# Matmul, causal mask and softmax: longer runs over four batches, and the mask read as 2.5 KB runs behind the weight

## The chip, the cores and the metric

The kernel runs on one core of a Trainium2 chip. The metric is the device time of one execution in microseconds (us); lower is better. Ten executions of the kernel before took 90.90 to 91.21 us, median 90.98. A profile of one execution (90.9 us) gives the instructions of each engine and the work of the core's 16 DMA engines.

Names: TensorE (PE) multiplies, and its weight loads are listed apart (PEld); VectorE is DVE, ScalarE is ACT, GpSimd is POOL, SyncE is SP. In this kernel every DMA is issued by SP, so all of them stand in one queue.

## The reference

```python
batch, m, k, n = 16, 512, 512, 512
x = randn(16, 512, 512); weight = randn(512, 512); scale = 0.125
mask = (np.triu(np.ones((m, n))) == 0)      # 1 strictly below the diagonal

y = scale * np.matmul(x, weight)
y = np.where(mask == 1, y, -1e9)
y_exp = np.exp(y - np.max(y, axis=-1, keepdims=True))
out = y_exp / np.sum(y_exp, axis=-1, keepdims=True)
```

All tensors are float32 in memory. x and the output are 16 MB each, the weight is 1 MB, and so is the whole mask. Row r of a batch has r columns that count. The first row of each batch has none, so its softmax is 1/512 everywhere. For rows 0 to 255 the right half of the columns is masked out entirely.

## The kernel before, in words

**Units.** The work is cut into 16 units. A unit holds half of the rows (h = 0: rows 0 to 255, h = 1: rows 256 to 511) of two neighbouring batches. Each of its 128 partitions holds four neighbouring rows of one batch, a run of 8 KB in memory. So a unit's x tile is 1 MB, its output tile too. Units alternate between h = 0 and h = 1.

**Steps of a unit.** `load` (L78) reads the x tile. `cast` (L83) turns it to bf16 on DVE. `transpose` (L88) makes 16 transposes of 128x128 on PE into two PSUM tiles. `evict` (L101) copies one of them to SBUF on DVE and the other on ACT. `multiply` (L108) does, for each of four row slots, four matmuls with the bf16 weight and a fifth one that adds a band of the mask (an identity times `band`, L127); then ACT takes the exponential and the row's sum. For h = 0 only the left 256 columns are computed; the right half of those output tiles was zeroed once at the start. `normalise` (L148) divides on DVE, and POOL writes 1/512 to the first rows. `store` (L158) writes the output tile.

**The band.** The mask matters only in the four 128x128 squares on its diagonal. At the start these are read into `diag_f32`, one mask row of each square to a partition, as 512 pieces of 512 bytes. DVE turns ones and zeros into 0 and -512 (`diag_bf`, L194). Four matmuls with `spread` (L208) bring the rows to the partitions and slots where the units have them, and DVE and ACT copy them into `band` (L215), 256 columns wide.

**Order.** `seq` keeps the program's order on each engine. SP issues x of unit 0, the mask squares, the weight, then x of units 1 to 7. PE runs 12 matmuls on zeros first. Unit 0 is cast, transposed and evicted, the band is made, the weight is cast. Then the loop over u follows: transpose(u+1), cast(u+2), evict(u+1), multiply(u), normalise(u-1), store(u-1), and the load of unit u+7 into the x buffer that has come free. There are eight x buffers and eight output buffers of 8 KB a partition, three buffers each for the bf16 x and its transpose, and four PSUM banks for each of the two uses.

Of the kernel before, what the change touches and what calls it, by code (L numbers as in the profile page):

```python
# [8 lines left out]
FP32 = mybir.dt.float32  # L9
BF16 = mybir.dt.bfloat16  # L10
AF = mybir.ActivationFunctionType
ALU = mybir.AluOpType

MASK_NEG = -512.0
P = 128
X_BUFS = 8
OUT_BUFS = 8
WARM = 12


@with_exitstack
def kernel(
    ctx: ExitStack,
    tc: tile.TileContext,
    x: bass.AP,
    weight: bass.AP,
    scale: float,
    mask: bass.AP,
    out: bass.AP,
):  # L30

    nc = tc.nc

    B, M, K = x.shape
    K2, N = weight.shape
    assert K == K2 and N == 512 and K == 512 and M == 512 and B % 2 == 0
    KT = K // P
    T = 4
    HP = P // 2
    HB = 2 * P
    U = B  # L50

    const = ctx.enter_context(tc.tile_pool(name="const", bufs=1))
    x_pool = ctx.enter_context(tc.tile_pool(name="xf", bufs=X_BUFS))
    xb_pool = ctx.enter_context(tc.tile_pool(name="xb", bufs=3))
    xt_pool = ctx.enter_context(tc.tile_pool(name="xt", bufs=3))
    sum_pool = ctx.enter_context(tc.tile_pool(name="sums", bufs=4))
    psum_t = ctx.enter_context(tc.tile_pool(name="psum_t", bufs=4, space=bass.MemoryType.PSUM))
    psum_y = ctx.enter_context(tc.tile_pool(name="psum_y", bufs=4, space=bass.MemoryType.PSUM))

    x_r = x.rearrange("(c e) (h p t) k -> c h p e (t k)", e=2, h=2, t=T)  # L60
    out_r = out.rearrange("(c e) (h p t) n -> c h p e (t n)", e=2, h=2, t=T)

    diag_r = bass.AP(tensor=mask.tensor, offset=mask.offset, ap=[[N, P], [P * N + P, KT], [1, P]])

    ident_bf = const.tile([P, P], BF16, name="ident_bf")
    w_f32 = const.tile([P, KT, N], FP32, name="w_f32")
    w_bf = const.tile([P, KT, N], BF16, name="w_bf")
    diag_f32 = const.tile([P, KT, P], FP32, name="diag_f32")
    diag_bf = const.tile([P, KT, P], BF16, name="diag_bf")
    spread = const.tile([P, T, P], BF16, name="spread")  # L70
    zeros = const.tile([P, N], BF16, name="zeros")
    band = const.tile([P, 2, T, HB], BF16, name="band")
    ots = [const.tile([P, T, N], FP32, name=f"ot{i}") for i in range(OUT_BUFS)]

    st_x, st_xb, st_pt, st_xt, st_sum = {}, {}, {}, {}, {}
    seq = tc.keep_in_program_order

    def load(u):  # L78
        xf = x_pool.tile([P, T, K], FP32, name="xf")
        seq(nc.sync.dma_start(xf.rearrange("p t k -> p (t k)"), x_r[u // 2, u % 2]))  # L80
        st_x[u] = xf

    def cast(u):  # L83
        xb = xb_pool.tile([P, T, K], BF16, name="xb")
        seq(nc.vector.tensor_copy(xb, st_x.pop(u)))  # L85
        st_xb[u] = xb

    def transpose(u):  # L88
        xb = st_xb.pop(u)
        st_pt[u] = [psum_t.tile([P, 2, T, P], BF16, name="pt") for _ in range(2)]  # L90
        for kt in range(KT):
            for t in range(T):
                seq(
                    nc.tensor.transpose(  # L94
                        st_pt[u][kt // 2][:, kt % 2, t],
                        xb[:, t].rearrange("p (k kt) -> p kt k", kt=KT)[:, kt],
                        ident_bf,
                    )
                )

    def evict(u):  # L101
        xt = xt_pool.tile([P, KT, T, P], BF16, name="xt")
        pt = st_pt.pop(u)
        seq(nc.vector.tensor_copy(xt[:, 0:2], pt[0]))  # L104
        seq(nc.scalar.copy(xt[:, 2:4], pt[1]))  # L105
        st_xt[u] = xt

    def multiply(u):  # L108
        h = u % 2
        NC = (h + 1) * HB  # L110
        xt = st_xt.pop(u)
        ot = ots[u % OUT_BUFS]
        rsum = sum_pool.tile([P, T], FP32, name="rsum")
        for t in range(T):
            py = psum_y.tile([P, N], FP32, name="py")
            for kt in range(KT):
                seq(
                    nc.tensor.matmul(  # L118
                        py[:, :NC],
                        lhsT=xt[:, kt, t],  # L120
                        rhs=w_bf[:, kt, :NC],
                        start=(kt == 0),
                        stop=(kt == KT - 1),
                    )
                )
            seq(
                nc.tensor.matmul(  # L127
                    py[:, h * HB : NC],
                    lhsT=ident_bf,
                    rhs=band[:, h, t],  # L130
                    start=False,
                    stop=True,
                    skip_group_check=True,
                )
            )
            seq(
                nc.scalar.activation(  # L137
                    out=ot[:, t, :NC],
                    in_=py[:, :NC],
                    func=AF.Exp,  # L140
                    bias=0.0,
                    scale=float(scale),
                    accum_out=rsum[:, t : t + 1],
                )
            )
        st_sum[u] = rsum

    def normalise(u):  # L148
        ot = ots[u % OUT_BUFS]
        NC = (u % 2 + 1) * HB  # L150
        rinv = sum_pool.tile([P, T], FP32, name="rinv")
        seq(nc.vector.reciprocal(rinv, st_sum.pop(u)))  # L152
        for t in range(T):
            seq(nc.vector.tensor_scalar_mul(ot[:, t, :NC], ot[:, t, :NC], rinv[:, t : t + 1]))  # L154
        if u % 2 == 0:
            seq(nc.gpsimd.memset(ot[0:2, 0, :HB], 1.0 / N))  # L156

    def store(u):  # L158
        ot = ots[u % OUT_BUFS]
        seq(nc.sync.dma_start(out_r[u // 2, u % 2], ot.rearrange("p t n -> p (t n)")))  # L160


    load(0)
    seq(nc.sync.dma_start(diag_f32, diag_r))  # L164
    seq(nc.sync.dma_start(w_f32, weight.rearrange("(p kt) n -> p kt n", kt=KT)))  # L165
    for u in range(1, X_BUFS):
        load(u)


    nc.vector.memset(zeros, 0.0)  # L170
    idle = psum_y.tile([P, N], FP32, name="py")
    for _ in range(WARM):
        seq(nc.tensor.matmul(idle, lhsT=zeros[:, :P], rhs=zeros, start=True, stop=True))  # L173

    make_identity(nc, ident_bf)
    nc.gpsimd.memset(band[:HP, :, :, P:], MASK_NEG)
    nc.gpsimd.memset(band[HP:, :, :, :P], 0.0)
    for i in range(0, OUT_BUFS, 2):
        nc.vector.memset(ots[i][:, :, HB:], 0.0)  # L179
        nc.gpsimd.memset(ots[i][0:2, 0, HB:], 1.0 / N)  # L180


    for g in range(2):
        for e in range(2):
            seq(
                nc.scalar.copy(  # L186
                    spread.rearrange("k t (g p e) -> k t g p e", g=2, e=2)[:, :, g, :, e],
                    ident_bf.rearrange("k (p t) -> k t p", t=T),
                )
            )  # L190

    cast(0)
    seq(
        nc.vector.tensor_scalar(  # L194
            out=diag_bf,
            in0=diag_f32,
            scalar1=-MASK_NEG,
            scalar2=MASK_NEG,
            op0=ALU.mult,
            op1=ALU.add,  # L200
        )
    )
    transpose(0)
    evict(0)
    for t in range(T):
        pm = psum_y.tile([P, N], FP32, name="py")
        seq(
            nc.tensor.matmul(  # L208
                pm, lhsT=spread[:, t], rhs=diag_bf.rearrange("k b c -> k (b c)"), start=True, stop=True
            )  # L210
        )
        for g, copy in enumerate((nc.vector.tensor_copy, nc.scalar.copy)):
            half = slice(g * HP, (g + 1) * HP)
            src = pm.rearrange("p (h g c) -> p h g c", h=2, g=2)
            seq(copy(band[half, :, t, g * P : (g + 1) * P], src[half, :, g]))  # L215
    seq(nc.vector.tensor_copy(w_bf[:, 0:2], w_f32[:, 0:2]))
    seq(nc.scalar.copy(w_bf[:, 2:4], w_f32[:, 2:4]))
    cast(1)

    for u in range(U + 1):  # L220
        if u + 1 < U:
            transpose(u + 1)
        if u + 2 < U:
            cast(u + 2)
        if u + 1 < U:
            evict(u + 1)
        if u < U:
            multiply(u)
        if u >= 1:
            normalise(u - 1)  # L230
            store(u - 1)
            if u - 1 + X_BUFS < U:
                load(u - 1 + X_BUFS)


# [33 lines left out]
```

The softmax here doesn't subtract the row's maximum and nothing guards it: scores larger than these inputs give would overflow.

## Time and profile before

| What | Value |
|---|---|
| Median of 10 executions | 90.98 us (90.90 to 91.21) |
| The profiled execution | 90.9 us |
| Its span, first to last instruction | 89.1 us |
| Busy: PE, DVE, ACT, POOL | 70.9, 60.4, 55.2, 7.3 us |
| Mean granted TensorE clock | 0.932 |
| DMA: bytes, mean rate over the span | 34.95 MB, 392 GB/s |
| x tiles: 16 loads of 1 MB, median from issue to landing | 14.2 us |
| Output: 16 stores of 1 MB, median from issue to landing | 11.0 us |
| Weight, 1 MB; mask squares, 256 KB: issue to landing | 8.5 us; 6.6 us |

The span leaves out what lies around the first and last instruction, 1.8 us in the profiled execution. In the page's slices a digit is a busy share in tenths. "DMA" is the mean busy share of the 16 DMA engines and "GB/s" what they moved in that slice. An issue-to-landing time includes the time in the queue behind other transfers.

### The profile page before, as it was taken

Reading aid. Unit: us, or ns where it says so; the run is one execution under the profiler, and the core shown is the slowest. Engines: PE = TensorE matmul, PEld = TensorE weight load, DVE = VectorE, ACT = ScalarE, POOL = GpSimd, SP = SyncE. Lnnn points to the kernel's source line nnn. Section 1 sums busy time; section 2 is a strip of 40 time slices with the busy share of each in tenths; the row PEclk is TensorE's granted clock in tenths of the full one; section 3 lists DMA queues with packets and bytes.
Section 4 is the critical chain, followed back from the end, with each engine's and each line's share of the span. In section 5 each row is a group of like instructions: output and inputs, shape, how many; then the busy total and the mean of one; then the engine's idle time right before and its main releaser. Section 6 shows DMA issues by size and latency. Waiting matters only on the chain.

```text
span 89.1 us, 1610 instructions
## 1 busy us (share of the span) xinstructions
PE 70.9 (80%) x584; PEld 49.1 (55%) x592; DVE 60.4 (68%) x123; ACT 55.2 (62%) x154; POOL 7.3 (8%) x20
## 2 busy tenths in 40 slices
PE   4966205999999999999999999999999999930000
PEld 1315005776598479659857964984796497400000
DVE  5875914758579949986994998698593976535000
ACT  5402930658687869687786977778787778650000
POOL 7620000002000200010020002002000100200000
PEclk9999975579999999999999999999999999999855
DMA  0969999999999999999999999999999999999960
GB/s 15 313 211 377 430 438 416 419 434 427 419 412 419 434 427 423 430 404 430 419 430 427 427 412 434 427 423 430 427 423 419 434 416 434 416 434 427 430 294 29
DMA packets 5286, 34.95 MB, mean 392 GB/s; under 512 B 544, under 2 KB 1056, under 8 KB 1056
## 3 DMA queue, kind: packets, MB, share of 16 engines
q1 hardware_dynamic: 5280, 34.87, 94.1%
q8 instruction: 4, 0.07, 0.3%
q14 instruction: 2, 0.02, 0.0%
HBM read 18.09 MB, written 16.78 MB: 391 GB/s over the span
## 4 chain that ended last, share of the span: by engine, by line
PE 72%; DMA 12%; DVE 3%; SPq 2%; issue 1%; ACT 1%; DVEq 0%; ACTq 0%
PE py L118 48%; PE pt L94 16%; DMA xf<-in_x_dram 12%; PE py L127 8%; DVE ot L154 1%; DVE xb L85 1%; SPq L80 1%; ACT ot L137 1%; SPq L164 1%; SPq L165 1%; DVEq L264 0%; DVE rinv L152 0%; ACTq L264 0%
## 5 line engine op out<-in xcount | busy, mean ns | idle before, releaser
L118 PE MATMUL py<-w_bf,xt 128*128 128x256 bf16 (+1 forms) x248 | 50.4, 331 | 0.4
L137 ACT ACTIVATE ot<-py 128x256 f32<-128x256 f32 (+1 forms) x64 | 31.2, 494 | 8.4 <-PE py L127 8.1
L118 PEld LDWEIGHTS <-xt 128*128 128x128 bf16 x256 | 25.0, 100 | 12.6
L105 ACT COPY xt<-pt 128x1024 bf16<-128x1024 bf16 x16 | 16.2, 1012 | 14.8 <-PE pt L94 10.2
L85 DVE CAST xb<-xf 128x2048 bf16<-128x2048 f32 x16 | 19.5, 1220 | 7.0 <-DMA xf<-in_x_dram 7.0
L154 DVE TENSOR_SCALAR ot<-ot,rinv 128x256 f32<-128x256 f32 (+1 forms) x64 | 23.5, 431 | 0.8
L94 PE MATMUL pt<-ident_bf,xb 128*128 128x128 bf16 x256 | 17.8, 225 | 6.0 <-DVE xb L85 6.0
L94 PEld LDWEIGHTS <-xb 128*128 128x128 bf16 x256 | 16.6, 115 | 7.8 <-DVE xb L85 6.9
L127 PE MATMUL py<-band,ident_bf 128*128 128x256 bf16 x64 | 17.7, 277 | 0.0
L104 DVE COPY xt<-pt 128x1024 bf16<-128x1024 bf16 x16 | 11.0, 687 | 7.4 <-PE pt L94 7.4
L137 ACT ACTIVATION_READ_ACCUMULATOR ot<-py 128x1 f32 x64 | 12.8, 200 | 0.0
L156 POOL MEMSET ot<- 2x256 f32 x8 | 3.6, 448 | 67.1 <-DVE ot L154 67.1
L127 PEld LDWEIGHTS <-ident_bf 128*128 128x128 bf16 x64 | 6.4, 100 | 4.3
L173 PE MATMUL py<-zeros 128*128 128x512 bf16 x12 | 4.8, 583 | 1.2 <-DVE zeros L170 1.2
L152 DVE RECIPROCAL rinv<-rsum 128x4 f32<-128x4 f32 x16 | 2.7, 169 | 3.2 <-ACT ot L137 3.2
L179 DVE MEMSET ot<- 128x1024 f32 x4 | 3.6, 912 | 0.6 <-issue 0.6
L173 PEld LDWEIGHTS <-zeros 128*128 128x128 bf16 x12 | 1.6, 140 | 3.9 <-issue 2.7
L186 ACT ACT_TABLE_LOAD x1 | 1.3, 1283 | 0.7 <-PEq L250 0.7
L215 ACT CAST band<-py 64x256 bf16<-64x256 f32 x4 | 1.4, 367 | 0.1
L215 DVE CAST band<-py 64x256 bf16<-64x256 f32 x4 | 1.4, 404 | 0.0
L180 POOL MEMSET ot<- 2x256 f32 x4 | 1.2, 302 | 1.5 <-DVE ot L179 1.4
L208 PE MATMUL py<-diag_bf,spread 128*128 128x512 bf16 x4 | 1.0, 377 | 0.3 <-DVE diag_bf L194 0.3
(14 smaller groups left out, 6.6 us busy)
## 6 DMA issues: line engine op xcount, KB each, us to landing
xf<-in_x_dram SPq DMA_DIRECT2D x16, 1024.0 KB, 14.2
out_dram<-ot SPq DMA_DIRECT2D x16, 1024.0 KB, 11.0
w_f<-in_weight_dram SPq DMA_DIRECT2D x1, 1024.0 KB, 8.5
diag_f<-in_mask_dram SPq DMA_DIRECT2D x1, 256.0 KB, 6.6
```

Of the source, the lines that this page charges most:

```text
L85: seq(nc.vector.tensor_copy(xb, st_x.pop(u)))
L94: nc.tensor.transpose(st_pt[u][kt // 2][:, kt % 2, t], xb[:, t].rearrange("p (k kt) -> p kt k", kt=KT)[:, kt], ident_bf,)
L104: seq(nc.vector.tensor_copy(xt[:, 0:2], pt[0]))
L105: seq(nc.scalar.copy(xt[:, 2:4], pt[1]))
L118: nc.tensor.matmul(py[:, :NC], lhsT=xt[:, kt, t], rhs=w_bf[:, kt, :NC], start=(kt == 0), stop=(kt == KT - 1),)
L127: nc.tensor.matmul(py[:, h * HB : NC], lhsT=ident_bf, rhs=band[:, h, t], start=False, stop=True, skip_group_check=True,)
L137: nc.scalar.activation(out=ot[:, t, :NC], in_=py[:, :NC], func=AF.Exp, bias=0.0, scale=float(scale), accum_out=rsum[:, t : t + 1],)
L154: seq(nc.vector.tensor_scalar_mul(ot[:, t, :NC], ot[:, t, :NC], rinv[:, t : t + 1]))
L156: seq(nc.gpsimd.memset(ot[0:2, 0, :HB], 1.0 / N))
L173: seq(nc.tensor.matmul(idle, lhsT=zeros[:, :P], rhs=zeros, start=True, stop=True))
L179: nc.vector.memset(ots[i][:, :, HB:], 0.0)
L215: seq(copy(band[half, :, t, g * P : (g + 1) * P], src[half, :, g]))
```

## The change

- A tile now holds eight neighbouring rows to a partition, a run of 16 KB, over four neighbouring batches: 2 MB for one h. A unit of compute is still 1 MB: four of the eight row slots of a tile. So two units with h = 0 are followed by two with h = 1. All x tiles but the first are loaded as one transfer of 2 MB; the first in two halves. All output tiles but the first and last are stored as one transfer, after the second unit; those two in halves. There are five x buffers and four output buffers, each of 16 KB a partition; the bf16 x and its transpose have two buffers instead of three.
- The queue at the start: first half of x tile 0, weight, second half of x tile 0, mask, then x tiles 1 to 4. The mask had been second.
- The mask is read in four transfers, one for each square. Each reads 64 runs of 2.5 KB: the 128 columns of one mask row, then on through memory to the 128 columns of the next row. Sixteen partitions get four runs each. The data lie for that time in the last output buffer. In all 640 KB are read instead of 256 KB, and into 64 partitions instead of 128.
- The band has two DVE conversions of 64 partitions (even and odd rows), four matmuls with a smaller `spread`, and eight copies of 64 partitions by 512 elements. It is made after units 0 and 1 were transposed and evicted, and after 14 and 8 more matmuls on zeros.

```diff
-X_BUFS = 8
-OUT_BUFS = 8
+X_BUFS = 5
+OUT_BUFS = 4
...
+    E = 4
+    S = 8
     T = 4
...
-    xb_pool = ctx.enter_context(tc.tile_pool(name="xb", bufs=3))
-    xt_pool = ctx.enter_context(tc.tile_pool(name="xt", bufs=3))
+    xb_pool = ctx.enter_context(tc.tile_pool(name="xb", bufs=2))
+    xt_pool = ctx.enter_context(tc.tile_pool(name="xt", bufs=2))
...
-    x_r = x.rearrange("(c e) (h p t) k -> c h p e (t k)", e=2, h=2, t=T)
-    out_r = out.rearrange("(c e) (h p t) n -> c h p e (t n)", e=2, h=2, t=T)
-    diag_r = bass.AP(tensor=mask.tensor, offset=mask.offset, ap=[[N, P], [P * N + P, KT], [1, P]])
+    x_r = x.rearrange("(c e) (h p t) k -> c h p e (t k)", e=E, h=2, t=S)
+    out_r = out.rearrange("(c e) (h p t) n -> c h p e (t n)", e=E, h=2, t=S)
...
-    load(0)
-    seq(nc.sync.dma_start(diag_f32, diag_r))
+    load(0, slots(0))
     seq(nc.sync.dma_start(w_f32, weight.rearrange("(p kt) n -> p kt n", kt=KT)))
-    for u in range(1, X_BUFS):
-        load(u)
+    load(0, slots(1))
+    DP = P // S
+    RUN = N + P
+    diag_f32 = ots[OUT_BUFS - 1].rearrange("p t n -> p (t n)")[:HP, : S // 2 * RUN]
+    for b in range(KT):
+        seq(
+            nc.sync.dma_start(
+                diag_f32[b * DP : (b + 1) * DP],
+                bass.AP(
+                    tensor=mask.tensor,
+                    offset=mask.offset + b * P * (N + 1),
+                    ap=[[2 * N, P // 2], [1, RUN]],
+                ),
+            )
+        )
+    for g in range(1, X_BUFS):
+        load(g)
...
     cast(0)
-    seq(nc.vector.tensor_scalar(out=diag_bf, in0=diag_f32, ...))
     transpose(0)
+    spin(14)
     evict(0)
-    for t in range(T):
...
     seq(nc.vector.tensor_copy(w_bf[:, 0:2], w_f32[:, 0:2]))
     seq(nc.scalar.copy(w_bf[:, 2:4], w_f32[:, 2:4]))
     cast(1)
+    transpose(1)
+    spin(8)
+    evict(1)
+    for side in range(2):
+        seq(nc.vector.tensor_scalar(out=diag_bf[... side], in0=diag_f32[... side * N : side * N + P], ...))
+    for h in range(2):
+        for j in range(2):
...
...
-            store(u - 1)
-            if u - 1 + X_BUFS < U:
-                load(u - 1 + X_BUFS)
+            g, second = divmod(u - 1, 2)
+            if g in (0, G - 1):
+                store(g, slots(u - 1))
+            elif second:
+                store(g)
+            if second and g + X_BUFS < G:
+                load(g + X_BUFS)
```

## The prediction

> **What bounds the kernel now.** I began with the page: the span, the engines' shares and the slices.
>
> ```profile
> span 89.1 us, 1610 instructions
> ...
> PE 70.9 (80%) x584; PEld 49.1 (55%) x592; DVE 60.4 (68%) x123; ACT 55.2 (62%) x154; POOL 7.3 (8%) x20
> ...
> DMA  0969999999999999999999999999999999999960
> GB/s 15 313 211 377 430 438 416 419 434 427 419 412 419 434 427 423 430 404 430 419 430 427 427 412 434 427 423 430 427 423 419 434 416 434 416 434 427 430 294 29
> ...
> q1 hardware_dynamic: 5280, 34.87, 94.1%
> ```
>
> TensorE is busy for four fifths of the span, but the transfer engines are never free between the start and the last slices, except in slice 2. The table by stage gives the rates (columns: length, busy time and count of five engines, TensorE clock, DMA share, GB/s).
>
> ```profile
> 5.00:7.00 2.00, 0.99 (x4) 0.25 (x2) 1.54 (x2) 0.00 (x0) 0.30 (x1) 1.00 0.48 129
> 7.00:12.00 5.00, 2.11 (x20) 1.26 (x20) 3.15 (x8) 3.42 (x6) 0.00 (x0) 1.00 1.02 424
> 12.00:24.00 12.00, 9.62 (x69) 7.01 (x71) 7.46 (x11) 5.59 (x15) 0.45 (x1) 0.72 1.02 425
> 24.00:44.00 20.00, 19.90 (x196) 15.26 (x196) 16.50 (x35) 16.15 (x49) 0.89 (x2) 1.00 1.01 423
> 44.00:64.00 20.00, 19.84 (x172) 13.79 (x173) 16.30 (x36) 15.59 (x44) 1.35 (x3) 1.00 1.01 426
> ```
>
> From 7 us on the rate is about 424 GB/s whatever the engines do. The hole from 5 to 7 us is the mask: 512 pieces of 512 B, 258 KB in 2 us. The timeline dates the landings, because each cast at the start waits for its x tile (start, duration, instruction, wait before it).
>
> ```profile
> 5.89 1.23 DVE L85 CAST xb<-xf 128x2048 bf16<-128x2048 f32 x1 [0.46 <-DMA xf<-in_x_dram]
> ...
> 8.05 0.43 DVE L194 TENSOR_SCALAR diag_bf<-diag_f 128x512 bf16<-128x512 f32 x1 [0.94 <-DMA diag_f<-in_mask_dram]
> ...
> 13.04 1.23 DVE L85 CAST xb<-xf 128x2048 bf16<-128x2048 f32 x1 [1.80 <-DMA xf<-in_x_dram]
> ...
> 15.52 1.23 DVE L85 CAST xb<-xf 128x2048 bf16<-128x2048 f32 x1 [1.25 <-DMA xf<-in_x_dram]
> ...
> 81.40 0.54 SPq L160 DMA_DIRECT2D out_dram<-ot  x1
> ```
>
> ```profile
> DMA to landing us min/median/max: 6.7/11.0/16.6
> ```
>
> The last line is of the stores; the last store has the minimum, so it lands at 81.40 + 6.7 = 88.1. One MB takes 15.52 - 13.04 = 2.5 us. The mask took 8.05 - 5.89 = 2.16. After it come 32 transfers of 1 MB (weight, 15 x tiles, 16 stores): 8.05 + 32 x 2.5 = 88.05. One unbroken chain of transfers explains the end to 0.1 us. The chain of waits names TensorE instead (72%): it reaches the last store's issue, not why that store needs 6.7 us; alone a first load needs 5.15 (issue 0.74, landed 5.89). The slack of the compute side is the difference, about 1.5 us.
>
> The trace's packet records give the finer law: an 8 KB packet takes 309 ns (median), a 512 B one 27. So a byte costs 282/7680 = 0.0367 ns (27.2 GB/s an engine) and a packet 27 - 18.8 = 8.2 ns besides.
>
> **What the Trainium skill says.** SBUF — State Buffer, Door 1: the DMA port swizzle: SBUF has 16 DMA ports of about 27.2 GB/s, each for eight fixed partitions; a tile on partitions 0 to 15 reaches four ports, measured at 104 GB/s, asymptote 109, and one on 128 reaches all. Same page, "Can I just issue two DMAs to hit both halves?": two transfers to different partitions gained 6% together. DMA: Bandwidth & Descriptors, Why a DMA increments its semaphore by 16 and not by 1: the engines used are the largest divisor up to 16 common to both sides' slowest dimension; 64 source rows and 16 partitions give 16. The trace of before agrees with 27.2 GB/s an engine, but has only 128-partition transfers: no row shows the four-port rate. TensorE: Matmul & The Clock Gate, Part 1: after an idle window of about 3.4 us the clock halves; here the clock was 0.72 over 12 to 24 us, after TensorE had idled from 9.55 to 14.3.
>
> **The change part by part, along the transfer queue.**
>
> *Mask.* Removed: 2.16 us. Added: four transfers of 64 runs of 2,560 B, each into 16 partitions, 655,360 B. By packets alone: 16 per engine x (8.2 + 94) = 1.64 us, the low end. By the skill's port price (an estimate): four engines share each port, so each transfer takes 163,840 B / 109 GB/s = 1.5 us, four take 6.0; at 104 GB/s 6.3, the high end. They lie in one queue, which an engine works off in order, so engines in step use four ports at a time. I take 6.0. If neighbouring transfers (different ports, for partitions 0 to 15 and 16 to 31) overlapped wholly, 3.0.
>
> *Longer runs.* Seven x tiles and six stores become 2 MB of 16 KB runs. Each engine has 8 packets fewer per pair, 8 x 8.2 = 66 ns, and one completion fewer (9 ns), so 2 MB takes 5.00 - 0.08 = 4.92 us; 13 of them save 1.0 us. If long runs were cut into 8 KB packets, nearly nothing; I take 1.0.
>
> *Sum.* Landings: x0 first half 5.89 (unchanged, 8 KB runs), weight +2.5, second half +2.5 = 10.9, mask +6.0 = 16.9, thirteen 2 MB transfers +64.0, four 1 MB stores +10.0: 90.85. Against 88.1 that is +2.75, or (mask - 3.25). The profiled execution is 90.9 us, 1.8 above its span and 2.8 above the last landing; so 93.65, and on the median of 90.98, **93.7 us**.
>
> *Issue.* SyncE spends about 0.6 us on each issue; the mask has three more, moved behind the weight and the second half of x0. They are covered by the 3 MB ahead (7.5 us); uncovered they'd cost 1.8.
>
> *Compute at the start.* The mask lands at 16.9 instead of 8.05. The two mask conversions (0.43 each, as L194) end at 17.8; behind them on VectorE stand the band copies, cast(2) and every later evict. Four spread matmuls (0.25 each at the full clock) and four copies per engine of twice the 0.40 and 0.37 us elements, near 0.6 each, let multiply(0) run at about 18.9 to 21. Transposes 0 and 1, the weight cast, and 22 spin matmuls lie in the wait for DMA: free. The next x tile lands whole at 16.9 + 4.92 = 21.8, cast until 23.0, so transpose(2) starts there and multiply(1) is queued behind it on TensorE. From 23.0, with the before rates (transposing a unit 0.89; multiplying 2.1 for a left-half unit and 3.9 for a full one): multiply(1) 2.1, two lots of transposes 1.8, then multiply 2 to 15 (8 x 3.9 + 6 x 2.1) and 12 lots of transposes (10.7): end near 81.5. Two left-half units in a row ask about 3.3 us of VectorE and ScalarE against 3.0 of TensorE, but two full ones follow, and four PSUM banks carry 0.6 us.
>
> *Compute at the end.* Before, the last matmul ended at 78.9 and the store was issued 2.5 us later. So issue near 84.0, alone landed by 84.0 + 5.15 = 89.2, 1.7 before the queue gets to 90.85: hidden. Without that cover each later microsecond counts in full.
>
> *Merged stores.* A first unit's output waits for its neighbour, up to 3.9 us of TensorE. The first merged store comes at about 39 us, when loads and the two first halves still fill the queue to 46 (21.8 + 3 x 4.9 + 5.0 + 4.9); later it grows. Fewer, larger buffers hold as much as before for output (64 KB a partition) and more for x (80 against 64); x7 lands at 66, needed at 70; xb and xt at two buffers still let a cast stand one unit ahead. I cost these, the memsets and the spread at nothing: they lie under the queue; without that cover a store late by a unit would cost 3.9.
>
> **The rivals.**
>
> *Ports don't bind* (not slower): an engine writes any partition at 27.2 GB/s. The mask then takes 1.64, the last landing is 86.5, 1.6 earlier: 89.4 us. For it: no row of before shows port sharing, and 2.5 KB packets need no more than 102 ns. Against: the measured 104 GB/s in the skill. It decides when the four transfers take less than 3.25 us, above 200 GB/s.
>
> *Port groups overlap:* mask 3.0 us, end -0.25: 90.7. For: transfers alternate between two sets of ports. Against: engines in step and in order, and the 6%.
>
> *Compute exposed:* the mask late and TensorE idle from the last spin (near 14.7) to 17.8, and again at 21 to 23. If the clock halves there, as it did after 3 us of idling (TensorE stopped at 9.55, clock 0.5 from 12.6), re-warming took until about 19 from 14.3: 4.8 us at half rate, 2.4 lost. The last store is then issued at 86.4 and lands at 91.5: 94.4 us, to 95.2 if half of the left-half units' 0.3 us excess is not caught up.
>
> **How the numbers follow.** Queue with four-port mask, compute hidden: 0.64, 93.7, own range 92.8 to 94.3. Compute exposed: 0.13, 94.4. Overlapping ports: 0.11, 90.7. Ports not binding: 0.12, 89.4. The range must hold 8 in 10: the first two hold 0.77, so the third is taken in: 90.5 to 95.2, leaving out the fourth and a tail. A change under 0.2% (0.18 us) can't be told from none. Faster: 0.12 and half of the third, 0.17; same 0.04; slower 0.79.
>
> **What would show it.** Right: the DMA rate falls to near 109 GB/s for about 6 us after 3 MB; the mask conversion waits until about 17; from then on the share is full and the rate rises by about 1% (near 429); the last store is issued with over 6 us to its landing. Wrong: the conversion starts by 13 us (ports don't bind), or at 14 (overlap); no fall in packet number (5,280) would undo the 1.0 us; holes in the DMA share after 20 us would mean that merged stores or the x buffers starve the queue; a last store landing 5.2 us after its issue would mean that compute sets the end.

## The result, and the profile after

The changed kernel takes 94.1 us in the median of 8 executions (93.82 to 94.84), against 90.97 before: 1.0355 times as long, 95% interval 1.0338 to 1.0373. The prediction was 93.7. The profiled execution took 93.85 us, with a span of 91.9; worked out for it were 93.65 and 91.85. Now and then an execution falls into a slower state with a lower granted clock (one with the extra transfers to 128 partitions below took 97.86 us at 0.819, its other three 92.56 to 92.69), and the ratios leave such executions out.

From the page of the changed kernel (busy tenths and GB/s in 40 slices; the queue):

```profile
span 91.9 us, 1628 instructions
...
PEclk9999999966999999999999999999999999999955
DMA  1999999999999999999999999999999999999970
GB/s 29 367 392 442 263 137 246 435 414 406 442 442 428 385 449 399 438 417 446 424 442 399 442 414 449 421 406 442 435 421 413 435 428 456 421 392 428 421 296 25
...
q1 hardware_dynamic: 3200, 35.26, 95.2%
```

The transfer engines are busy in every slice, slices 4 to 6 (counted from 0: from 9.2 to 16.1 us) included; there they are busy and move little. The table by stage shows the two sides of it: a busy share of more than 1 at a third of the rate while the mask is read, and full rates otherwise.

```profile
7.00:9.00 2.00, 1.77 (x20) 1.32 (x21) 1.27 (x3) 0.65 (x1) 0.00 (x0) 1.00 1.02 430
...
11.00:12.00 1.00, 0.34 (x2) 0.00 (x0) 0.14 (x1) 0.00 (x0) 0.00 (x0) 1.00 1.07 141
12.00:13.00 1.00, 0.00 (x0) 0.00 (x0) 1.00 (x1) 0.00 (x0) 0.00 (x0) 1.00 1.07 138
13.00:14.00 1.00, 0.86 (x15) 0.86 (x16) 0.27 (x2) 0.00 (x0) 0.00 (x0) 1.00 1.29 167
...
24.00:44.00 20.00, 19.84 (x184) 14.82 (x186) 17.04 (x39) 16.14 (x47) 0.90 (x2) 1.00 1.01 427
44.00:64.00 20.00, 19.90 (x177) 14.02 (x178) 16.26 (x36) 15.71 (x45) 0.45 (x1) 1.00 1.00 425
```

The mask of before left the engines half idle (share 0.48 at 129 GB/s). This is the opposite: engines that hold packets and can't finish them. The packet records say the same: of the 256 packets of 2,560 B the first 46, but for one, took 100 to 102 ns, and the median of all is 287.

The timeline gives the landings, as before through the instructions that wait for them, and the list of stores the end:

```profile
5.95 1.23 DVE L88 CAST xb<-xf 128x2048 bf16<-128x2048 f32 x1 [0.53 <-DMA xf<-in_x_dram]
...
11.86 1.23 DVE L88 CAST xb<-xf 128x2048 bf16<-128x2048 f32 x1 [2.66 <-DMA xf<-in_x_dram]
...
16.63 0.75 DVE L223 TENSOR_SCALAR diag_bf<-ot 64x512 bf16<-64x512 f32 x2 [2.12 <-DMA ot<-in_mask_dram]
...
21.27 2.36 DVE L88 CAST xb<-xf 128x2048 bf16<-128x2048 f32 x2 [0.95 <-DMA xf<-in_x_dram]
```

```profile
L164 SPq DMA_DIRECT2D out_dram<-ot x10: 538/549/616, 25.8 to 84.7; - x10
...
DMA to landing us min/median/max: 6.4/12.3/17.2
```

From the first half tile (5.95) to the next whole tile (21.27) are 15.3 us. Two transfers of 1 MB (5.0) and one of 2 MB (4.9) leave 5.4 for the mask. The second half of the first tile landed at 11.86, about 0.9 later than its place in the queue (5.95 + 5.0): some engines were then at the mask's packets already. Where the mask goes to 32 or 128 partitions (below), the same way takes 5.48 and 4.93 us instead of 5.91, so the delay belongs to the mask's form. The last store lands at 84.7 + 6.4 = 91.1. From 21.27 that is 69.8 us for twelve transfers of 2 MB and four of 1 MB, so 4.98 for 2 MB where 4.92 was predicted and 5.00 is twice the old 1 MB.

### The profile page after: what moved, and what is told of

Its sections match the earlier page's. It is cut to its first block, busy times and chain, and to the rows that moved or that the text cites. A ratio compares the mean times of both kernels' runs of the same rounds, so it can differ in the third digit from the quotient of the medians.

```text
span 91.9 us, 1628 instructions
## 1 busy us (share of the span) xinstructions
PE 75.1 (82%) x606; PEld 50.5 (55%) x614; DVE 61.1 (67%) x122; ACT 55.8 (61%) x154; POOL 6.6 (7%) x14
## 4 chain that ended last, share of the span: by engine, by line
PE 68%; DMA 13%; SPq 4%; DVE 3%; ACT 1%; issue 1%; DVEq 0%; ACTq 0%
PE py L121 46%; PE pt L97 14%; DMA ot<-in_mask_dram 13%; PE py L130 8%; SPq L178 2%; DVE ot L157 1%; SPq L84 1%; DVE diag_bf L223 1%; DVE band L247 1%; ACT ot L140 1%; ACT band L247 1%; SPq L168 1%; DVEq L301 0%; PE py L236 0%; DVE rinv L155 0%
## 5 line engine op out<-in xcount | busy, mean ns | idle before, releaser
L97 PE MATMUL pt<-ident_bf,xb 128*128 128x128 bf16 x256 | 17.0, 219 | 3.0 <-DVE xb L88 3.0
L196 PE MATMUL py<-zeros 128*128 128x512 bf16 x33 | 9.7, 454 | 1.2 <-DVE zeros L191 1.2
L196 PEld LDWEIGHTS <-zeros 128*128 128x128 bf16 x34 | 3.7, 112 | 6.0 <-issue 2.7
L159 POOL MEMSET ot<- 4x256 f32 x4 | 1.8, 448 | 65.6 <-DVE ot L157 65.6
L247 ACT CAST band<-py 64x512 bf16<-64x512 f32 x4 | 2.3, 580 | 3.3 <-DVE band L247 3.3
L204 DVE MEMSET ot<- 128x2048 f32 x2 | 3.5, 1765 | 0.7 <-issue 0.7
L247 DVE CAST band<-py 64x512 bf16<-64x512 f32 x4 | 2.5, 676 | 0.5 <-PE py L236 0.5
L236 PE MATMUL py<-diag_bf,spread 64*128 64x512 bf16 x4 | 1.0, 374 | 1.5 <-DVE diag_bf L223 1.5
L223 DVE TENSOR_SCALAR diag_bf<-ot 64x512 bf16<-64x512 f32 x2 | 0.8, 414 | 2.1 <-DMA ot<-in_mask_dram 2.1
L202 POOL MEMSET band<- 64x2048 bf16 x1 | 1.8, 1799 | 0.1
```

What stands on the lines that cost most here:

```text
L97: nc.tensor.transpose(st_pt[u][kt // 2][:, kt % 2, t], xb[:, t].rearrange("p (k kt) -> p kt k", kt=KT)[:, kt], ident_bf,)
L247: copy(band[half, h, slots(j), g * P : (g + 1) * P], pm.rearrange("p (t c) -> p t c", t=T)[half],)
```

## The experiments

Four theories were to be told apart. **Ports**, as the prediction has them: 16 partitions reach four SBUF ports, so four engines share each. **Short runs**: pieces of 2.5 KB are slow wherever they land. **Compute**: the late band, not the queue, sets the end. And, for the second term of the sum, what **long runs** are worth.

### The mask's transfers alone, in the kernel before

The cleanest test adds the 640 KB to the kernel before, behind the weight and the second x tile, into a buffer that nobody reads. The two runs differ in where the same 256 runs land (and in being four transfers or two, which the next pair of versions tells apart).

```diff
+    extra = const.tile([HP, T * (N + P)], FP32, name="extra")
+    for b in range(KT):     # 16 partitions each
+        seq(nc.sync.dma_start(extra[b * 16 : (b + 1) * 16],
+            bass.AP(tensor=mask.tensor, offset=mask.offset + b * P * (N + 1), ap=[[2 * N, P // 2], [1, N + P]])))
```

> The kernel before with four more transfers in its queue, behind the weight and the second x tile: the changed kernel's 640 KB of mask in the changed kernel's form (16 partitions each), into a buffer that nobody reads. The cost of these transfers by itself, in a kernel with none of the other edits. Port theory, from the stage that the changed kernel showed (5.4 us): 91.0 + 5.4 = 96.4. If ports don't bind and packets alone count: 91.0 + 1.6 = 92.6. If TensorE's chain set the end and not the queue: under 1 us more, because the work would wait only at the start.

```diff
+    extra = const.tile([P, 2 * (N + P)], FP32, name="extra")
+    for r in range(2):      # 128 partitions each
+        seq(nc.sync.dma_start(extra[:, r * (N + P) : (r + 1) * (N + P)],
+            bass.AP(tensor=mask.tensor, offset=mask.offset + 2 * N * r,
+                    ap=[[4 * N, P // 4], [P * (N + 1), KT], [1, N + P]])))
```

> The kernel before with the same 640 KB and the same 256 runs of 2.5 KB at the same place, but spread over all 128 partitions (two transfers). Port theory alone: 1.7 us more, 92.7. Port theory with a second term, a hole of about 1.3 us that short packets leave in the queue (2.9 us of stage in the run with 128 partitions, and 2.16 for the mask of before against 0.9 of packets): 2.9 us more, 93.9. Short-run theory without ports: the same as with 16 partitions.

Measured: 96.63 us on 16 partitions (ratio 1.0618, 1.0599 to 1.0637) and 92.65 on 128 (1.0178, 1.0160 to 1.0197), against 90.97 for the kernel before beside them: 5.7 and 1.7 us more. The stages of the two, first 16 partitions, then 128 (in both, the window lies in the extra transfers but for the last few packets of x ahead of them):

```profile
12.00:17.00 5.00, 1.40 (x14) 1.41 (x15) 1.23 (x1) 0.00 (x0) 0.00 (x0) 0.57 1.13 167
```

```profile
12.00:13.00 1.00, 0.00 (x0) 0.00 (x0) 0.02 (x1) 0.00 (x0) 0.00 (x0) 1.00 0.95 379
```

Same bytes, same runs, same place, both times busy engines: 167 against 379 GB/s. In the packet records the 2.5 KB packets to 128 partitions have a median of 102 ns (the longest took 114), the price that the prediction had worked out; to 16 partitions their median is 299. With the version on 32 partitions below, this settles that the destination partitions make the price; and the mask's form alone costs more than the whole change lost. The hole of 1.3 us that the second expectation added didn't appear here (more below).

### The changed kernel with the mask on more partitions

The layout of the mask rows over partitions is changed, and with it the spread matrices (one for each pair of half and slot group); the band and all that follows stay.

```diff
-    for b in range(KT):     # four transfers, 16 partitions, 4 runs each
-        ... diag_f32[b * DP : (b + 1) * DP], ap=[[2 * N, P // 2], [1, RUN]]
+    for r in range(2):      # two transfers, 128 partitions, 1 run each
+        ... diag_f32[:, r * RUN : (r + 1) * RUN], ap=[[4 * N, P // 4], [P * (N + 1), KT], [1, RUN]]
```

> The changed kernel with one thing different: the same 640 KB of mask, in the same 256 runs of 2.5 KB and at the same place in the queue, go to all 128 partitions (two transfers of 128 runs) instead of 64 (four transfers of 16 partitions). Port theory (16 partitions reach four of 16 SBUF ports, so four engines share each): the mask stage falls from the 5.4 us that the landings show (second x tile at 21.3, first half tile at 5.95, less 2 x 2.5 and 4.9) to 1.7, the mask conversion starts by about 13, the time is 94.1 - 3.7 = 90.4. Rival, short runs (2.5 KB pieces from separate rows are slow whatever they land on): no change, 94.1. Rival, compute sets the end: little change, over 93.

The other version keeps the four transfers of the changed kernel, but each goes to 32 partitions with two runs:

```diff
-    DP = P // S
+    DP = P // KT            # four transfers, 32 partitions, 2 runs each
```

> As the kernel with 128 partitions, but four transfers, each into 32 neighbouring partitions with two runs each: eight ports by the skill's table, so two engines to a port. Port theory: mask stage near 2.9 us, between the two others, time near 91.6. Short-run theory: as the changed kernel, 94.1. If the number of transfers counted and not the ports (four here as in the changed kernel, two with 128 partitions): 94.1 too.

Measured: 91.75 (ratio to the kernel before 1.0087, 1.0050 to 1.0125) and 91.49 (1.0076, 1.0045 to 1.0108). From the changed kernel's 94.1 these are gains of 2.35 and 2.6. So the short-run theory and the number of transfers are out: the second version has as many transfers, with the same runs, and gains as much as 128 partitions do. The packet records fit shared ports: the median of a 2,560 B packet is 102 ns to 128 partitions, 180 to 32 and 287 to 16, where one, two or four engines sharing 27.2 GB/s would need 94, 188 and 376. No run took 16 partitions from 16 different ports, so it isn't shown that the ports, and not the mere number of partitions, are what is shared. But 128 partitions were expected to gain 3.7. The landings of the two versions say why, first those with 128 partitions:

```profile
6.13 1.23 DVE L88 CAST xb<-xf 128x2048 bf16<-128x2048 f32 x1 [0.71 <-DMA xf<-in_x_dram]
...
18.99 2.36 DVE L88 CAST xb<-xf 128x2048 bf16<-128x2048 f32 x2 [1.11 <-DMA xf<-in_x_dram]
```

```profile
5.76 1.23 DVE L88 CAST xb<-xf 128x2048 bf16<-128x2048 f32 x1 [0.34 <-DMA xf<-in_x_dram]
...
18.92 2.37 DVE L88 CAST xb<-xf 128x2048 bf16<-128x2048 f32 x2 [0.78 <-DMA xf<-in_x_dram]
```

18.99 - 6.13 - 5.0 - 4.9 = 2.95 us of mask, where packets alone would take 1.7 (with 32 partitions 3.2, where the ports give 2.9 to 3.0). So with 128 partitions something adds 1.3 us that is not the ports, and with 32, where the ports alone take that long, next to nothing is added; it is also in the mask of before, which took 2.16 for 32 packets of 27 ns an engine, 0.9.

### What adds 1.3 us to the mask

Pieces of 512 B on 128 partitions move less. The tile layout is the one of the version before, read in four transfers of 128 pieces:

```diff
-    for r in range(2):
-        ... ap=[[4 * N, P // 4], [P * (N + 1), KT], [1, RUN]]
+    for t in range(T):
+        ... ap=[[4 * N, P // 4], [P * (N + 1), KT], [1, P]]
```

> The changed kernel with the mask on 128 partitions and read as 512 B pieces (256 KB in four transfers of 128 pieces) at the same place in the queue. With the hole of 1.3 us and packets of 27 ns, 32 per engine (0.9): stage 2.2 us, 0.7 less than with 2.5 KB runs on 128 partitions, 91.0. If 512 B pieces were worse than 2.5 KB runs, over 91.75.

Measured 90.85, ratio 0.9995 (0.9973 to 1.0018): as expected, and level with the kernel before.

Then the queue. In the kernel before the mask's transfer is given to another queue:

```diff
-    seq(nc.sync.dma_start(diag_f32, diag_r))
+    seq(nc.scalar.dma_start(diag_f32, diag_r))
```

> The kernel before with one word different: the mask's transfer is issued by ScalarE, so it stands in another queue beside the x tiles and not between them. If the hole that short packets leave is waiting and not work of the engines, x packets fill it: the mask costs 0.9 instead of 2.16, 91.0 - 1.3 = 89.7. If the hole is work of the engines or of memory, no change.

Measured: twelve executions from 90.31 to 94.07, median 91.56, where those of the kernel before beside them lie from 90.84 to 91.11. The fastest seven, up to 91.60, have a ratio of 1.0011 (0.9977 to 1.0044), so even they show no gain. In the profile the first x tile landed at 8.95 instead of 5.89, with the small packets now beside it in the start; between 2 and 5 us only 185 GB/s were moved. So the time was lost at the start instead. That doesn't decide what the hole is.

The run with extra transfers to 128 partitions reads mask rows that the kernel had read before, and had no hole. So a first access to the mask tensor was the next suspect. A tiny read of 16 mask rows, issued by ScalarE at the start, should then take the hole away:

```diff
+    touch = const.tile([16, 16], FP32, name="touch")
+    seq(nc.scalar.dma_start(touch, bass.AP(tensor=mask.tensor, offset=mask.offset, ap=[[32 * N, 16], [1, 16]])))
```

It was added to the kernel before, to the version with 512 B pieces and to the one with 2.5 KB runs on 128 partitions.

> The kernel before plus one tiny transfer issued by ScalarE at the start: 64 B from each of 16 mask rows, 32 rows apart, into a tile that nobody reads. It asks whether the hole in the mask's stage (2.16 us for 0.9 of packets) belongs to the first read of the mask: the second read of it, in the run with extra transfers to 128 partitions, had no hole. If a first access to the tensor anywhere opens it: 91.0 - 1.3 = 89.7. If the hole is of the rows themselves, or of short packets: 91.0, or up to 0.2 more.

> The same tiny early transfer added to the changed kernel with 512 B pieces on 128 partitions. First-access theory: the queue ends 1.3 us earlier, but the last store's issue at 81 and its 5.2 us leave only 1.5 to 2 of slack, so 89.5 to 89.9 against 90.85 without. Otherwise 90.9.

> The same tiny early transfer added to the changed kernel with 2.5 KB runs on 128 partitions. First-access theory: mask stage from 2.9 to 1.7 us, 91.75 - 1.2 = 90.5. Otherwise 91.75.

Measured: 91.09 (1.0022, 1.0011 to 1.0033), 91.19 (1.0016, 1.0003 to 1.0029) and 91.36 (1.0041, 1.0025 to 1.0058). The first became slower by 0.2 us; the second isn't faster than its 90.85 without. The third is 0.4 below its 91.75, with intervals that overlap, and not 1.2; its way from the first half tile to the next whole tile (5.81 to 18.59) is 12.78 us, and was 12.86 without the touch. In the first the mask's conversion starts at the old time:

```profile
5.86 1.23 DVE L85 CAST xb<-xf 128x2048 bf16<-128x2048 f32 x1 [0.42 <-DMA xf<-in_x_dram]
8.02 0.43 DVE L196 TENSOR_SCALAR diag_bf<-diag_f 128x512 bf16<-128x512 f32 x1 [0.93 <-DMA diag_f<-in_mask_dram]
```

8.02 - 5.86 = 2.16, to the hundredth what it was. The theory of a first access to the tensor falls. What is left is that it belongs to the first read of those very rows, or to something else that the second read doesn't share; no run tells these apart, so it stays open. It isn't a fixed cost either: to 16 partitions the first read took 5.4 us (in the changed kernel) and the second 5.7 (in the kernel before).

### The queue or compute

Without the mask's transfers (the buffer filled with ones on GpSimd, so this kernel leaves out the masking inside the diagonal squares):

```diff
-    for b in range(KT):
-        seq(nc.sync.dma_start(diag_f32[b * DP : (b + 1) * DP], ...))
+    nc.gpsimd.memset(diag_f32, 1.0)
```

> The changed kernel without the mask's transfers: the mask buffer is filled with ones on GpSimd instead, so nothing inside the diagonal squares is masked out. What the transfers cost in all. Port theory with the queue as the bound: 94.1 - 5.4 = 88.7. Compute as the bound: a smaller gain, because the band could be made at 12 us already but TensorE's work of over 60 us stays; if it set the end, near 91.

Measured 90.41 (0.9948, 0.9925 to 0.9970): 3.7 us gained, not 5.4. Its stores and its last stages:

```profile
L164 SPq DMA_DIRECT2D out_dram<-ot x10: 538/539/614, 23.4 to 82.0; - x10
...
DMA to landing us min/median/max: 5.4/12.2/16.2
```

```profile
80.00:82.00 2.00, 0.00 (x0) 0.00 (x0) 1.85 (x5) 0.06 (x1) 0.00 (x0) 1.00 0.99 414
82.00:84.00 2.00, 0.00 (x0) 0.00 (x0) 0.00 (x0) 0.00 (x0) 0.00 (x0) 0.66 0.71 299
```

The last store is issued at 82.0 and lands 5.4 later. That looks as if compute set the end, since a first load alone took 5.15. The trace's landing records, one for each of the 16 engines, say otherwise. Eleven engines had finished all else (hence the share of 0.71) and landed their part of the last store from 86.05 to 86.22, 4.0 to 4.2 us after its issue. The other five landed the store before only from 84.0 to 85.0, and the last one about 2.4 us later each, the last at 87.4: that is the time of one transfer, so they had no pause. The queue set the end here too, on its slowest engines.

Why 3.7, then, and not 5.4? In this profile there is a stretch from 24 to 34 us at 356 GB/s with a full share, where packets of 16 KB took about 1.1 us instead of 0.61. It costs 1.6 us of transfer time, which is the difference; I can't explain it, and whether the other executions had it isn't known. Without it the end would have come near 86.2, where the eleven engines had it, and compute would have set it (an estimate). The fill took part in that: with GpSimd writing, the first cast took 2.42 us instead of 1.23, so the band was no earlier than in the version on 128 partitions. This run bounds the price of the mask from below; the pair in the kernel before measures it.

Without the later matmuls on zeros:

```diff
     transpose(0)
-    spin(14)
     evict(0)
...
     transpose(1)
-    spin(8)
     evict(1)
```

> The changed kernel without the 14 and 8 matmuls on zeros between the first transposes (the first 12 stay). They stand under the wait for the mask. If the queue sets the end and compute has 1.1 us of slack (last store issued at 84.67, landed 6.4 later, against 5.3 alone): 94.1, up to 95 if the halved clock lasts 2 us longer. If the clock at the start set the time, 95.5 and more.

Measured 94.15 (1.0355, 1.0335 to 1.0376), the changed kernel's own ratio. Its stores, a stage with the halved clock, and the next whole tile after the mask:

```profile
L164 SPq DMA_DIRECT2D out_dram<-ot x10: 539/548/621, 27.5 to 86.4; - x10
...
DMA to landing us min/median/max: 5.3/12.0/16.0
```

```profile
13.00:18.00 5.00, 1.95 (x17) 1.79 (x18) 1.69 (x4) 1.01 (x1) 0.00 (x0) 0.50 1.07 270
```

```profile
21.72 2.36 DVE L88 CAST xb<-xf 128x2048 bf16<-128x2048 f32 x2 [0.68 <-DMA xf<-in_x_dram]
```

The clock was at half from 11.5 to 25.2 us (in the changed kernel from 19.0 to 22.4), and the last store was issued 1.7 us later than in the changed kernel. It landed at 91.7 instead of 91.1 in these two profiles. But the queue was 0.45 us behind already at 21.7 (21.27 in the changed kernel), and no load up to there waits for TensorE. At the end its slowest engine again went from the store before (landed at 89.3) to the last without a pause. So the cover at the end, the time by which the queue outlasts compute, was not used up, and the medians agree. The 22 matmuls hide in the wait for the mask and buy nothing that can be measured.

### Long runs

The version with the mask on 128 partitions, with each 2 MB transfer issued as two of 1 MB and 8 KB runs:

```diff
-        run = slice(part.start * K, part.stop * K)
-        seq(nc.sync.dma_start(... [:, run], x_r[g // 2, g % 2][:, :, run]))
+        for i in range(part.start, part.stop, T):
+            run = slice(i * K, (i + T) * K)
+            seq(nc.sync.dma_start(... [:, run], x_r[g // 2, g % 2][:, :, run]))
     # the same in store
```

> The kernel with the mask on 128 partitions, but every 2 MB transfer issued as two of 1 MB with 8 KB runs. What long runs are worth. The packet law of the prediction (8.2 ns for each packet saved, 13 pairs): 1.0 us slower than with long runs, 91.4. The rates of the two profiles in their steady stages (424.5 and 426 GB/s between 40 and 80 us; the DMA share of 1.01 before says that neighbouring packets overlap): 0.3 us slower, 90.7.

Measured 92.12 (1.0135, 1.0109 to 1.0161) against 91.75 (1.0087, 1.0050 to 1.0125): long runs gain about 0.4 us, with intervals that just overlap, so the size is rough. The two profiles' own rates between 40 and 80 us, 426 and 422 GB/s, give 0.6 over the whole queue. (The rates in the expectation are those of 24 to 64 us.) The 1.0 of the packet law is too much.

No version that keeps the mask beats both kernels. The best, with 512 B pieces on 128 partitions, is level with the kernel before.

## Why the prediction was right

**What bounds the kernel.** The unbroken chain of transfers was the right reading: the end of the changed kernel follows from its landings in the same way, and the engines' share has no hole after 20 us. The first merged store came at 38.75 (39 was worked out) and starved nothing. One refinement: a transfer lands with its slowest engine, and at the end the engines were 2.3 us apart (the last store landed from 88.75 to 91.09).

**Mask.** Taken at 6.0 us by the port price of the Trainium skill (SBUF — State Buffer, Door 1: the DMA port swizzle: 109 GB/s for 16 partitions), measured 5.4 in the changed kernel and 5.7 alone. The low end, 1.64 by packets, is just what 128 partitions cost (1.7). So the choice between the two ends, which decided the sign, was right, and the price was 5 to 11% too high: 655,360 B in 5.4 us are 121 GB/s, not 109. The first mask packets ran at 102 ns while neighbours still wrote the x tile, and in the stage the rate was 138 to 208 GB/s (the higher ones with packets of the next tile in them); that engines which are not in step use more than four ports at a time would explain this, but is only argued.

**Longer runs.** This step was mis-sized: 1.0 us predicted, 13 times 0.08; the landings show 0.02 for each pair (0.3 us in all), the experiment 0.4 to 0.6. The rate rose from 423 and 426 GB/s to 427 and 425 (24 to 44 and 44 to 64 us), not to the 429 that was named as a sign. The term that failed is the 8.2 ns for each packet. It came from packet durations as if packets followed one another; but the DMA share of 1.01 in the very lines that I showed can be read as an overlap of 1%, 3 ns of 309, which would hide a part of it. No run tests that reading. Twelve pairs after 21.27 at 4.98 instead of 4.92 make 0.7 us.

**The sum.** 90.85 was the last landing predicted, 91.1 measured: mask 0.6 less, runs 0.7 more, start 0.06 more. Two errors of opposite sign made the total look better than its terms; that was luck.

**Issue.** The mask's extra issues cost nothing; SyncE had its x loads out by 12.4 us.

**Compute at the start and the end.** Predicted: conversion 16.9, first multiply 18.9 to 21, transpose(2) at 23.0, last matmul 81.5, last store 84.0. Measured: 16.63, 19.2 to 23.1, 22.9, 82.0, 84.7. The clock did halve, from 19.0 to 22.4 us; it slowed only multiply(0), which held transpose(2) for some 0.4 us after its tile was cast. The Trainium skill (TensorE: Matmul & The Clock Gate, Part 1) led one to fear this after an idle window of about 3.4 us. Here less was enough: TensorE had been busy for 1.4 of the 3.4 us before 19.0, and in the kernel before the clock halved at 12.2 (the prediction says 12.6), 2.6 us after TensorE's last matmul.

The cover at the end was mis-sized, on the safe side: 1.7 us, with 5.15 for a store alone. Engines that had nothing ahead of a store landed it in 4.0 to 4.2 us, so 84.7 + 4.2 = 88.9, and the cover was about 2.2. That decides on the rival of exposed compute. It let TensorE lose 2.4 us to the halved clock, so that the last store is issued at 86.4; the run without the later matmuls had its last store at 86.4, and the queue still set its end.

**The rivals.** Ports don't bind: refuted by the pair in the kernel before. Overlapping port groups at 3.0 us: refuted (5.4), though with 32 partitions, eight ports, the stage was 3.2. Compute exposed: refuted as above.

## What to carry to other kernels

In a kernel that lives at the transfer engines' rate, a small load costs what its slowest resource costs for all engines: 1.8% of the bytes, on 16 partitions at a time, took 6% of the time. Spread even small loads over more partitions (32 at a time were as good as 128 here); longer runs don't make up for fewer partitions. Don't price a packet by its recorded duration alone: of the 1.0 us worked out in this way, 0.3 to 0.6 came. And before you call the end of a kernel compute's, look whether all transfer engines waited for the last store, or only some.

## What the runs showed of the hardware that was not expected

- A packet of 16 KB takes 611 ns and one of 8 KB 309 in the packet records, 7 ns less for two; in the queue 2 MB took 4.98 us against 5.00, 0.02 less, where eight such packets would save 0.06 on each engine.
- Packets of one form (2,560 B) took 102 ns to 128 partitions, 180 to 32 and about 290 to 16 in the median, with the engines counted as busy. A low rate at a full share was the mark of it here (it is not proof: the stretch without the mask at 356 GB/s had it too). The mask of before, at a share of 0.48, has another cause.
- The first read of the mask's rows to 128 partitions left about 1.3 us in which engines were idle or slow, in 512 B and in 2.5 KB pieces; a second read of the same rows did not. Where the destination was the limit, next to nothing was added (32 partitions: 3.2 us, of which 3.0 are the ports'). Reading 16 rows of the tensor ahead didn't change it. The cause is open.
- The tile ahead of the port-bound transfers landed late too (11.86 against 10.95).
- The engines don't end together: the last store of the changed kernel landed from 88.75 to 91.09, that of the kernel before from 85.97 to 88.12.
